# Seven products in place of eight for part of the gate and up projections of a decoder block

## The chip, the cores and the metric

The kernel runs as one launch on one core of a Trainium2 chip. The metric is the device time of one execution in microseconds (us), the median over several runs. The hardware profiler records one execution; its "span" runs from the first instruction to the last. Engines are named as the profile names them: PE is TensorE (matmul), PEld its weight loads, DVE is VectorE, ACT is ScalarE, POOL is GpSimd, SP is SyncE, whose queue issues most DMA transfers.

## The reference

One decoder layer over 256 tokens with 2048 features in float32: a mixer (state space heads and short convolutions), a cross-attention to 256 memory tokens, and a SwiGLU feed-forward network with 5632 hidden features, each with a norm ahead and a residual addition behind, and a final norm. The change is in the feed-forward network:

```
def swiglu(h, w_gate, w_up, w_down):
    return (jax.nn.silu(h @ w_gate) * (h @ w_up)) @ w_down
...
    h = h + swiglu(rmsnorm(h, norm_ffn[i]), w_gate[i], w_up[i], w_down[i])
return rmsnorm(h, norm_final)
```

## The kernel before

*Numbers.* Every float32 operand of a large product is split into a high part (rounded to fp32r) and a low part (what is left). A product is three matmuls: high by high, low by high, high by low. The weights are the moving operand (128 rows by 512 columns), 128x128 blocks of activations the stationary one, so every matmul is preceded by a weight load of an activation block.

*The stream of weights.* `stream_plan` lists all weight tiles in the order of use. A tile, called a chunk here, holds two blocks of 128 input features by 512 output features: 128x1024, 512 KB. Three steps move along that list: `load_to` issues the DMA into a ring of six raw tiles (line 151), `split_to` makes the high part on ScalarE (line 165) and the low part on VectorE (line 166) in rings of four tiles each, and `unit` writes out the matmuls of one or two chunks. `unit` loads up to six chunks ahead and splits up to two chunks past its own; after its first part it advances once each of the processes that are waiting (`step`).

*The order on the engines.* TensorE and SyncE execute in the order written. On ScalarE and VectorE a planner orders the instructions when the program is built; each engine then goes through its list in order.

*Feed-forward network.* The hidden features are in eleven blocks of 512 (`FN`), n = 0 to 10. A block needs eight chunks of the gate weights, `("g", n, c)`, and eight of the up weights, `("u", n, c)`, c = 0 to 7 being pairs of 128 input features. `tok_mm` writes twelve matmuls for a chunk: two feature blocks by two token halves (`tb`) by three, eight with the high weights (lines 238 and 239), then four with the low ones (line 242). They accumulate in PSUM in one bank of 128 tokens by 512 features for each token half; the pool `acc` has four banks, the pool `msc` four more. In blocks 1 to 10 the eight g chunks come first, then the eight u chunks. Two processes follow: `g_post` applies SiLU and the norm's scale on ScalarE, reading the banks (line 1035); `u_post` multiplies by the banks of u on VectorE (line 1043), transposes (line 257), writes the tile to memory (`put`, line 270), reads it back turned (`get`, line 277) and splits it into high and low parts for the down projection (lines 1053 and 1054). `put` and `get` stand in SyncE's queue between the weight loads.

The activations `h2g` are sixteen tiles of 128 features, 256 tokens high part and 256 low part. Those tiles, the finished gate tiles `gs`, the residual `res` and much else are of one size, 128x512 float32, in a pool of 63 called slots.

The down projection runs after block 10 through `d_mm`, also on `tok_mm`.

Of the kernel before, what the change touches and what calls it, by code (L numbers as in the profile page):

```python
# [10 lines left out]
F32 = mybir.dt.float32  # L14
F32R = mybir.dt.float32r
AF = mybir.ActivationFunctionType
ALU = mybir.AluOpType
# [3 lines left out]
T = 256  # L21
D = 2048
KT = D // 128
FF = 5632
FT = FF // 128
FN = FF // 512
H = 32
EPS = 1e-5
NEG = -3.0e38
# [34 lines left out]
            + [(n, c) for n in (2, 3) for c in range(KT)])  # L64


def ffn_order():

    return ([(m, 0, c) for h in range(2) for m in "gu" for c in range(4 * h, 4 * h + 4)]
            + [(m, n, c) for n in range(1, FN) for m in "gu" for c in range(KT // 2)])  # L70


def stream_plan():
# [14 lines left out]
def trunk(tc, wst, vecs, xp, xtp, mp, mtp, wdt_in, nfin, outp):  # L88
    nc = tc.nc
    plan = stream_plan()  # L90
    index = {k: i for i, (k, _) in enumerate(plan)}
    offs, o = [], 0
# [5 lines left out]
    with ExitStack() as ctx:  # L98
# [8 lines left out]
        bp = E(tc.tile_pool(name="blocks", bufs=2))  # L107
        fp = E(tc.tile_pool(name="feat", bufs=3))
# [8 lines left out]
        def nm(s):  # L117
            cnt[0] += 1
            return f"{s}{cnt[0]}"

        def slot(shape=(128, 512), dt=F32):
            return sp.tile(list(shape), dt, tag="s", name=nm("s"))
# [4 lines left out]
        def acc():  # L127
            return accp.tile([128, 512], F32, tag="a", name=nm("a"))

        def msc():  # L130
            return mscp.tile([128, 512], F32, tag="m", name=nm("m"))

        mm = nc.tensor.matmul
        act = nc.scalar.activation
        tt = nc.vector.tensor_tensor
        ts = nc.vector.tensor_scalar
        stt = nc.vector.scalar_tensor_tensor
# [6 lines left out]
        def load_to(n):  # L144
            while nload[0] < min(n, len(plan)):
                i = nload[0]
                w = plan[i][1]
                for f in before.pop(i, ()):
                    f()
                r = rawp.tile([128, 1024], F32, tag="r", name=nm("r"))  # L150
                nc.sync.dma_start(r[:, :w], wst[offs[i]:offs[i] + 128 * w].rearrange("(p n) -> p n", p=128))
                raws[i] = r
                nload[0] += 1

        def split_to(n):
            while nsplit[0] < min(n, len(plan)):
                i = nsplit[0]
                key, w = plan[i]
                r = raws.pop(i)
                h = hip.tile([128, 1024], F32R, tag="h", name=nm("h"))  # L160
                l = lop.tile([128, 1024], F32R, tag="l", name=nm("l"))
                m = 2 if i in (0, 2) else 1
                for j in range(m):
                    c = slice(j * w // m, (j + 1) * w // m)
                    nc.scalar.copy(h[:, c], r[:, c])  # L165
                    tt(l[:, c], r[:, c], h[:, c].bitcast(F32), ALU.subtract)  # L166
                los[i] = l
                his[i] = h
                nsplit[0] += 1
# [60 lines left out]
        def tok_mm(ps, key, blocks, tbs, start, stop, ks=(0, 1)):  # L230


            h, l = fin(key)
            for i in ks:
                w = slice(i * 512, i * 512 + 512)
                for tb in tbs:
                    ah, al = blocks(i, tb)
                    mm(ps[tb], ah, h[:, w], start=start and i == ks[0], stop=False)  # L238
                    mm(ps[tb], al, h[:, w], start=False, stop=False)  # L239
            for i in ks:  # L240
                for tb in tbs:
                    mm(ps[tb], blocks(i, tb)[0], l[:, i * 512:i * 512 + 512], start=False, stop=stop and i == ks[-1])  # L242

        def side_blocks(tiles, k0):

            def blocks(i, tb):
                a = tiles[k0 + i]
                hi, lo = a if isinstance(a, tuple) else (a[:, 0:T], a[:, T:])
                return hi[:, tb * 128:tb * 128 + 128], lo[:, tb * 128:tb * 128 + 128]

            return blocks

        def turn_blocks(src):

            t = bp.tile([128, 1024], F32, tag="b", name=nm("b"))
            for tb in range(2):
                nc.vector.transpose(t[:, tb * 512:tb * 512 + 512], src[tb])  # L257
            return t
# [8 lines left out]
        def put(t):  # L267

            w = drp.tile([2, 128, 512], F32, tag="w", name=nm("w"), bufs=2)
            nc.sync.dma_start(w.rearrange("t p k -> p t k"), t.rearrange("p (t k) -> p t k", t=2))  # L270
            return w
# [14 lines left out]
        def step():  # L286
            alive = []
            cur = list(procs)
            procs.clear()
            for p in cur:  # L290
                try:
                    next(p)
                    alive.append(p)
                except StopIteration:
                    pass
            procs[:0] = alive
# [9 lines left out]
        def unit(parts, post=None):  # L306

            first = [index[k] for k in parts[0][0]]
            last = max([index[k] for ks, _ in parts for k in ks])
            load_to(last + AHEAD - 1)  # L310
            split_to(last + 1)
            for i, (ks, fn) in enumerate(parts):
                fn()
                if i == 0:
                    step()
                    split_to(last + 3)
            load_to(last + AHEAD)
            if post is not None:
                procs.extend(post if isinstance(post, list) else [post])
            now[0] += 1  # L320

        def fin(key):
            i = index[key]
            return his[i], los.get(i)
# [59 lines left out]
        def until(u):  # L384
            while now[0] < u:
                yield
# [36 lines left out]

        dtn = cp.tile([128, 2, H], F32, name="dtn")
        nacs = cp.tile([128, 2, H], F32, name="nacs")
        scr = drp.tile([H, 384], F32, name="acsT")

        def dt_proc():


            yield from until(13)
            w3 = wdt.rearrange("p (k h) -> p k h", h=H)
            tt(w3, w3, vec[:, VOFF["nmix"]:VOFF["nmix"] + KT].unsqueeze(2).to_broadcast([128, KT, H]), ALU.mult)
            yield from until(15)
            ps = msc()
            for kt in range(KT):
                c = kt % 4
                mm(ps[32 * c:32 * c + 32, 0:T], wdt[:, kt * H:kt * H + H],  # L438
                   xraw[kt // 2][:, (kt % 2) * T:(kt % 2) * T + T], start=kt < 4, stop=kt >= 12)
# [98 lines left out]
        first = [[f(), f()] for f in (acc, msc)]  # L538
# [372 lines left out]
        for m, tiles in (("k", mh), ("q", h1g)):  # L911
            accs = [acc(), acc()]
# [57 lines left out]
        h2g = {}  # L970
        h2s = cp.tile([128, 2, 4], F32, name="h2s")
        ff = {}
# [31 lines left out]
        with tc.high_priority():  # L1004
            for mb in range(2):
                Vs.append(slot())
                c = scales["mem"][:, mb:mb + 1]
# [10 lines left out]
        for n in range(4):  # L1018
            accs = [acc(), acc()]
# [6 lines left out]
        gate = {}  # L1026
        gs = {}

        def g_post(n, accs):
            while "r" not in ff:  # L1030
                yield
            gate[n] = []
            for tb in range(2):
                s = gtp.tile([128, 512], F32, tag="g", name=nm("g"))
                act(s, accs[tb], AF.Silu, scale=ff["r"][:, tb:tb + 1])
                gate[n].append(s)

        def u_post(n, accs):
            while n not in gate:
                yield  # L1040
            for tb in range(2):
                s = gate[n][tb]
                stt(s, accs[tb], ff["r"][:, tb:tb + 1], s, ALU.mult, ALU.mult)  # L1043
            t = turn_blocks(gate[n])
            yield
            w = put(t)
            yield
            d = get(w)
            yield
            for i in range(2):  # L1050
                hi, lo = slot(dt=F32R), slot(dt=F32R)
                hv, lv = [a.rearrange("p (f x j) -> p f x j", f=2, x=8) for a in (hi, lo)]
                nc.scalar.copy(hv, d[:, 2 * i:2 * i + 2])  # L1053
                tt(lv, d[:, 2 * i:2 * i + 2], hv.bitcast(F32), ALU.subtract)  # L1054
                gs[2 * n + i] = hi, lo

        def f_mm(accs, m, n, c):
            tok_mm(accs, (m, n, c), side_blocks(h2g, 2 * c), (0, 1), c == 0, c == KT // 2 - 1)

        faccs = {}  # L1060
        order = ffn_order()
        for i in range(0, len(order), 2):
            m, n, c = order[i]
            if c == 0:
                faccs[m, n] = [acc(), acc()]
            parts = [([(m, n, k)], lambda k=k: f_mm(faccs[m, n], m, n, k)) for k in (c, c + 1)]
            p = (g_post if m == "g" else u_post)(n, faccs[m, n]) if c == KT // 2 - 2 else None
            if n == 0:
                unit(parts[:1])
                unit(parts[1:], p)  # L1070
            else:
                unit(parts, p)


        ss = cp.tile([128, 2, 5], F32, name="ss")
# [90 lines left out]
        for n in range(4):  # L1166
            accs = [acc(), acc()]
# [148 lines left out]
```

## Time and profile before

| | |
|---|---|
| median of 3 runs | 1510.32 us (1509.64 to 1510.48) |
| profiled execution, its own time | 1509.91 us |
| its span | 1508.2 us |
| TensorE, busy in the span | 99%, 6733 matmuls |
| VectorE, ScalarE, GpSimd | 61%, 51%, 2% |
| mean granted TensorE clock | 0.999 |
| DMA | 346.68 MB, mean 230 GB/s |

The share of busy time is an average over stages. In a line of a group, the source line, the engine and the operation come first, then the tile written and the tiles read with their shapes, the count, the busy time, the mean of one in ns, and behind the last bar the time in which the engine stood idle just before such an instruction, with what ended most of it. A TensorE matmul's busy time overlaps with that of its neighbours, so its cost is the distance from one start to the next and not the mean duration. In views in order of time a row has its start and its duration in us; several equal instructions in a row are drawn together (x2).

### The profile page before, as it was taken

The numbers are of one execution on the slowest core, as the hardware profiler recorded it, in microseconds if no ns is written. First come the engines' busy times: TensorE is split into PE (matmuls) and PEld (weight loads), VectorE is DVE, ScalarE is ACT, GpSimd is POOL, SyncE is SP. The second block draws the span as 40 slices with busy tenths as digits, with TensorE's granted clock in tenths as the row PEclk, the third lists the DMA queues.
The fourth block names the chain that finished last, engine by engine and source line by source line (L and its number), as shares of the span: only waits on it lengthen the run. The fifth ranks groups of instructions, "written<-read, shape, count | busy, mean of one in ns | idle before, by whom it ended". The sixth has DMA issues, their size and how long they took to land.

```text
span 1508.2 us, 18230 instructions
## 1 busy us (share of the span) xinstructions
PE 1497.8 (99%) x6733; PEld 1234.6 (82%) x6733; DVE 920.9 (61%) x1152; ACT 768.5 (51%) x1033; POOL 34.5 (2%) x46
## 2 busy tenths in 40 slices
PE   9999999999999999999999999999999999999997
PEld 7788888888888888888888888888888888888886
DVE  6677776777785765566675455555545555455453
ACT  7477554757654444454565444444444444344343
POOL 0011000101000000000000000000000000000000
PEclk9999999999999999999999999999999999999999
DMA  9786766868766766776557666666566667666662
GB/s 365 262 290 212 279 243 208 294 226 280 263 220 223 265 212 209 273 265 228 218 189 240 240 218 220 221 221 217 191 218 234 219 220 243 199 195 195 192 191 93
DMA packets 149210, 346.68 MB, mean 230 GB/s; under 512 B 11360, under 2 KB 62976, under 8 KB 149120
## 3 DMA queue, kind: packets, MB, share of 16 engines
q1 hardware_dynamic: 140064, 338.64, 65.7%
q10 hardware_dynamic: 9056, 6.87, 1.6%
q8 instruction: 52, 0.85, 0.2%
q14 instruction: 38, 0.31, 0.1%
HBM read 321.30 MB, written 24.17 MB: 229 GB/s over the span
## 4 chain that ended last, share of the span: by engine, by line
PE 98%; DMA 0%; issue 0%; DVE 0%; SPq 0%; ACT 0%; DVEq 0%; POOLq 0%; POOL 0%
PE a L238 32%; PE a L242 32%; PE a L239 32%; PE m L659 1%; PE m L238 0%; PE m L239 0%; PE m L242 0%; DMA r<-in_w_dram 0%; PE m L966 0%; PE m L661 0%; PE m L643 0%; PE m L935 0%; PE m L438 0%; PE m L954 0%; PE m L617 0%
## 5 line engine op out<-in xcount | busy, mean ns | idle before, releaser
L166 DVE TENSOR_TENSOR l<-r,h 128x1024 fp32r<-128x1024 f32 (+1 forms) x539 | 653.0, 1217 | 481.5 <-ACT h L165 471.4
L165 ACT CAST h<-r 128x1024 fp32r<-128x1024 f32 (+1 forms) x539 | 562.6, 1047 | 595.2 <-PE a L239 554.5
L238 PE MATMUL a<-h,s 128*128 128x512 f32 x2111 | 825.6, 391 | 0.0
L239 PE MATMUL a<-h,s 128*128 128x512 f32 x2111 | 821.8, 389 | 0.0
L242 PE MATMUL a<-l,s 128*128 128x512 f32 x2111 | 568.1, 389 | 0.1
L238 PEld LDWEIGHTS a<-h,s 128*128 128x128 f32 x2111 | 396.6, 188 | 84.3 <-issue 2.0
L242 PEld LDWEIGHTS a<-l,s 128*128 128x128 f32 x2111 | 396.2, 188 | 82.9 <-DVE l L166 0.5
L239 PEld LDWEIGHTS a<-h,s 128*128 128x128 f32 x2111 | 396.6, 188 | 81.3
L257 DVE STREAM_TRANSPOSE b<-s 128x512 f32<-128x512 f32 x62 | 40.6, 688 | 6.8 <-ACT s L264 6.8
L600 DVE SCALAR_TENSOR_TENSOR t<-t,vec,t 128x255 f32<-128x255 f32 (+2 forms) x72 | 32.9, 488 | 5.3 <-ACT t L597 4.6
L264 ACT ACTIVATE s<-a,xr 128x512 f32<-128x512 f32 x42 | 26.4, 680 | 4.0 <-DMA s<-acsT 3.5
L1043 DVE SCALAR_TENSOR_TENSOR g<-a,fscale,g 128x512 f32<-128x512 f32 x22 | 15.5, 746 | 12.0 <-PE a L242 12.0
L180 DVE SCALAR_TENSOR_TENSOR s<-s,vec,s 128x256 fp32r<-128x256 f32 x32 | 14.5, 479 | 5.9 <-ACT s L179 5.9
L815 ACT ACTIVATE s<-f,vec 128x256 fp32r<-128x256 f32 x28 | 12.2, 498 | 11.3 <-DMA f<-w 11.3
L1116 POOL TENSOR_TENSOR fr<-fr,half 128x1 f32<-128x1 f32 x2 | 1.1, 550 | 714.2 <-DVE fr L1115 714.2
L1054 DVE TENSOR_TENSOR s<-f,s 128x512 fp32r<-128x512 f32 x22 | 14.3, 687 | 3.7 <-ACT s L1053 2.5
L816 DVE SCALAR_TENSOR_TENSOR s<-f,vec,s 128x256 fp32r<-128x256 f32 x28 | 12.0, 480 | 7.1 <-ACT s L815 7.1
L582 ACT ACTIVATE s<-s,nacs 128x256 f32<-128x256 f32 x32 | 16.0, 500 | 0.0
L1053 ACT CAST s<-f 128x512 fp32r<-128x512 f32 x22 | 12.5, 618 | 6.5 <-DMA f<-w 6.5
L219 POOL TENSOR_TENSOR rr<-rv,half 128x2 f32<-128x2 f32 x8 | 6.5, 811 | 408.5 <-DVE rv L218 408.5
L179 ACT ACTIVATE s<-s,vec 128x256 fp32r<-128x256 f32 x32 | 15.2, 501 | 1.0 <-DMA s<-in_x_dram 0.4
L399 ACT ACTIVATE s<-s 128x512 f32<-128x512 f32 x16 | 10.1, 631 | 10.8 <-DMA s<-in_mt_dram 5.8
(171 smaller groups left out, 476.7 us busy)
## 6 DMA issues: line engine op xcount, KB each, us to landing
r<-in_w_dram SPq DMA_DIRECT2D x535, 512.0 KB, 4.3
w<-b SPq DMA_DIRECT2D x42, 512.0 KB, 3.3
f<-w SPq DMA_DIRECT2D x42, 512.0 KB, 5.1
s<-acsT ACTq DMA_DIRECT2D x24, 256.0 KB, 5.3
s<-in_xt_dram SPq DMA_DIRECT2D x16, 256.0 KB, 7.4
s<-in_mt_dram SPq DMA_DIRECT2D x8, 256.0 KB, 6.3
s<-in_m_dram SPq DMA_DIRECT2D x8, 256.0 KB, 3.9
s<-in_x_dram SPq DMA_DIRECT2D x7, 256.0 KB, 7.2
```

The source lines that it names most:

```text
L165: nc.scalar.copy(h[:, c], r[:, c])
L166: tt(l[:, c], r[:, c], h[:, c].bitcast(F32), ALU.subtract)
L179: act(a[:, 0:T], src, AF.Identity, scale=gain)
L238: mm(ps[tb], ah, h[:, w], start=start and i == ks[0], stop=False)
L239: mm(ps[tb], al, h[:, w], start=False, stop=False)
L242: mm(ps[tb], blocks(i, tb)[0], l[:, i * 512:i * 512 + 512], start=False, stop=stop and i == ks[-1])
L257: nc.vector.transpose(t[:, tb * 512:tb * 512 + 512], src[tb])
L264: act(o[tb], accs[tb], AF.Identity, scale=r[:, tb:tb + 1])
L582: act(t, t, AF.Exp, bias=b[:, 0:1])
L600: stt(a[:, d:], u[:, 0:T - d], v("cw", 4 * ct + k), a[:, d:], ALU.mult, ALU.add)
L659: mm(yp[64 * i:64 * i + 64, 0:T], xd[:, 0, i, :], f[:, i * T:i * T + T], start=True, stop=False)
L1043: stt(s, accs[tb], ff["r"][:, tb:tb + 1], s, ALU.mult, ALU.mult)
```

## The change

In blocks 1 to 7 (`SEVEN`), two of the eight feature pairs, c = 0 and c = 1, are treated otherwise. For one such pair, the activations are a two by two array of blocks (two feature blocks, two token halves) and the weights another (two feature blocks; g and u). Eight block products made up the result; now there are seven, of sums and differences of blocks, after Strassen's scheme (in Winograd's form), and the results are put together afterwards.

- `ffn_units` gives the new order. A block is: the pair c = 0 of g and u in one part; g2 g3 g4 u2 u3 u4 in three units of two chunks; the pair c = 1; g5 g6 g7 u5 u6 u7. The banks of g and u of a block are now both taken at its start.
- `token_sums` makes, once for each pair, the four sums of activation blocks and splits them into high and low parts (`seven_a`). It is written ahead of the ninth unit of block 0.
- `pair_sums`, called by `split_to` at the u chunk of a pair, makes four sums of weight halves on VectorE, in the raw tiles and one tile more, and splits three of them (128x512) into high and low parts on ScalarE and VectorE. One half of the u raw tile holds a sum when it is split as usual. The raw tile of g is held until then.
- `seven_mm` writes the 21 matmuls in three groups. Four of the products go to four banks of `msc` shared by both pairs, three directly to banks of g and u.
- `p_post` reads the four shared banks after the second pair: one copy on ScalarE, four additions or subtractions on VectorE, into two tiles of the pool `feat`. `whole` adds the result to a bank of g or u (one operation on VectorE for each of the four banks) before SiLU and before the product.

```
+SEVEN = range(1, 8)
...
+def ffn_units():
+    o = [[((m, 0, c),)] for h in range(2) for m in "gu" for c in range(4 * h, 4 * h + 4)]
+    for n in range(1, FN):
+        if n in SEVEN:
+            for q, rest in ((0, "g2 g3 g4 u2 u3 u4"), (1, "g5 g6 g7 u5 u6 u7")):
+                o.append([(("g", n, q), ("u", n, q))])
+                k = [(a[0], n, int(a[1])) for a in rest.split()]
+                o += [[(a,), (b,)] for a, b in zip(k[0::2], k[1::2])]
+        else:
+            o += [[((m, n, c),), ((m, n, c + 1),)] for m in "gu" for c in range(0, KT // 2, 2)]
+    return o
...
+        def pair_sums(nc_, u):
+            g = held.pop(nc_)
+            a, b = slice(0, 512), slice(512, 1024)
+            f = bp.tile([128, 1024], F32, tag="b", name=nm("b"))
+            tt(f[:, a], g[:, a], u[:, a], ALU.add)
+            tt(u[:, a], u[:, a], u[:, b], ALU.add)
+            tt(f[:, b], f[:, a], u[:, b], ALU.add)
+            tt(g[:, a], f[:, b], g[:, b], ALU.add)
+            pair_parts[nc_] = []
+            for x in (f[:, a], f[:, b], g[:, a]):
+                h, l = slot(dt=F32R), slot(dt=F32R)
+                nc.scalar.copy(h, x)
+                tt(l, x, h.bitcast(F32), ALU.subtract)
+                pair_parts[nc_].append((h, l))
...
+                if key in pairs:
+                    if key[0] == "g":
+                        held[key[1:]] = r
+                    else:
+                        pair_sums(key[1:], r)
                 h = hip.tile([128, 1024], F32R, tag="h", name=nm("h"))
...
+        def p_post(n, p):
+            x, y = [fp.tile([128, 1024], F32, tag="f", name=nm("f")) for _ in range(2)]
+            c11, c21, c12, c22 = x[:, 0:512], x[:, 512:], y[:, 0:512], y[:, 512:]
+            nc.scalar.copy(c11, p[0])
+            tt(c22, p[2], c11, ALU.subtract)
+            tt(c12, p[1], c22, ALU.add)
+            tt(c21, p[3], c22, ALU.add)
+            tt(c22, p[1], c21, ALU.add)
+            corr[n] = {("g", 0): (c11, ALU.add), ("g", 1): (c21, ALU.subtract),
+                       ("u", 0): (c12, ALU.add), ("u", 1): (c22, ALU.add)}
...
+        def whole(m, n, tb, ps):
+            if n not in SEVEN:
+                return ps
+            c, op = corr[n][m, tb]
+            tt(c, ps, c, op)
+            return c
...
-                act(s, accs[tb], AF.Silu, scale=ff["r"][:, tb:tb + 1])
+                act(s, whole("g", n, tb, accs[tb]), AF.Silu, scale=ff["r"][:, tb:tb + 1])
...
-                stt(s, accs[tb], ff["r"][:, tb:tb + 1], s, ALU.mult, ALU.mult)
+                stt(s, whole("u", n, tb, accs[tb]), ff["r"][:, tb:tb + 1], s, ALU.mult, ALU.mult)
...
+        def token_sums(c):
+            s0, s1 = h2g[2 * c], h2g[2 * c + 1]
+            x, y = slot(), slot()
+            for i, a in enumerate((s0, s1)):
+                tt(x[:, i * T:i * T + T], a[:, 0:T].bitcast(F32), a[:, T:].bitcast(F32), ALU.add)
+            a11, a21, a12, a22 = [x[:, i * 128:i * 128 + 128] for i in range(4)]
+            o = [y[:, i * 128:i * 128 + 128] for i in range(4)]
+            tt(o[0], a21, a22, ALU.subtract)
+            tt(o[1], a11, o[0], ALU.subtract)
+            tt(o[2], a21, a11, ALU.subtract)
+            tt(o[3], a12, o[1], ALU.subtract)
+            h, l = slot(dt=F32R), slot(dt=F32R)
+            nc.scalar.copy(h, y)
+            tt(l, y, h.bitcast(F32), ALU.subtract)
+            seven_a[c] = [(h[:, i * 128:i * 128 + 128], l[:, i * 128:i * 128 + 128]) for i in range(4)]
...
+        def seven_mm(n, c):
+            g, u, p = faccs["g", n], faccs["u", n], shared[n]
+            gh, gl = fin(("g", n, c))
+            uh, ul = fin(("u", n, c))
+            t1, t2, t4 = pair_parts.pop((n, c))
+            a, b = slice(0, 512), slice(512, 1024)
+            raw = side_blocks(h2g, 2 * c)
+            sa = seven_a[c]
+            for group in (((p[0], raw(0, 0), (gh[:, a], gl[:, a])), (g[0], raw(1, 0), (gh[:, b], gl[:, b]))),
+                          ((p[3], sa[2], (uh[:, a], ul[:, a])), (p[1], sa[0], t1)),
+                          ((p[2], sa[1], t2), (g[1], raw(1, 1), t4), (u[0], sa[3], (uh[:, b], ul[:, b])))):
+                for ps, (ah, al), (bh, bl) in group:
+                    mm(ps, ah, bh, start=c == 0, stop=False)
+                    mm(ps, al, bh, start=False, stop=False)
+                for ps, (ah, al), (bh, bl) in group:
+                    mm(ps, ah, bl, start=False, stop=c == 1 and any(ps is q for q in p))
...
+        for i, parts in enumerate(ffn_units()):
+            if i == 8:
+                for c in range(2):
+                    token_sums(c)
+            post = []
+            for part in parts:
+                m, n, c = part[0]
+                for k in part:
+                    if k[2] == 0:
+                        faccs[k[:2]] = [acc(), acc()]
+                if len(part) == 2:
+                    if c == 0:
+                        shared[n] = [msc() for _ in range(4)]
+                    else:
+                        post.append(p_post(n, shared[n]))
+                elif c == KT // 2 - 1:
+                    post.append((g_post if m == "g" else u_post)(n, faccs[m, n]))
+            unit([(list(part), lambda part=part: part_mm(part)) for part in parts], post or None)
```

More of the change, by code (lines that the diff above doesn't have):

```diff
@@ L64, in out_order @@
             + [(n, c) for n in (2, 3) for c in range(KT)])
+def ffn_units():
[9 more added lines that the diff above has]
+    return o
 def ffn_order():
-    return ([(m, 0, c) for h in range(2) for m in "gu" for c in range(4 * h, 4 * h + 4)]
-            + [(m, n, c) for n in range(1, FN) for m in "gu" for c in range(KT // 2)])
+    return [k for u in ffn_units() for part in u for k in part]
 def stream_plan():
@@ L153, in load_to @@
                 nload[0] += 1
+        held, pair_parts = {}, {}
+        pairs = {k for u in ffn_units() for part in u if len(part) == 2 for k in part}
+        def pair_sums(nc_, u):
[12 more added lines that the diff above has]
+                pair_parts[nc_].append((h, l))
         def split_to(n):
@@ L237, in tok_mm @@
                     ah, al = blocks(i, tb)
-                    mm(ps[tb], ah, h[:, w], start=start and i == ks[0], stop=False)
+                    first = start if isinstance(start, bool) else tb in start
+                    mm(ps[tb], ah, h[:, w], start=first and i == ks[0], stop=False)
                     mm(ps[tb], al, h[:, w], start=False, stop=False)
@@ L1027, in trunk @@
         gs = {}
+        corr = {}
+        def p_post(n, p):
[8 more added lines that the diff above has]
+                       ("u", 0): (c12, ALU.add), ("u", 1): (c22, ALU.add)}
+            return
+            yield
+        def whole(m, n, tb, ps):
[4 more added lines that the diff above has]
+            return c
         def g_post(n, accs):
@@ L1055, in u_post @@
                 gs[2 * n + i] = hi, lo
[L1057 to L1072, printed above, removed]
+        faccs, shared, seven_a = {}, {}, {}
@@ new lines, in part_mm @@
+        def part_mm(part):
+            m, n, c = part[0]
+            if len(part) == 2:
+                seven_mm(n, c)
+                return
+            start = c == 0
+            if n in SEVEN:
+                start = (1,) if (m, c) == ("u", 2) else False
+            tok_mm(faccs[m, n], part[0], side_blocks(h2g, 2 * c), (0, 1), start, c == KT // 2 - 1)
+        for i, parts in enumerate(ffn_units()):
[4 more added lines that the diff above has]
+            for part in parts:
+                m, n, c = part[0]
+                for k in part:
+                    if k[2] == 0:
+                        faccs[k[:2]] = [acc(), acc()]
+                if len(part) == 2:
+                    if c == 0:
[5 more added lines that the diff above has]
+            unit([(list(part), lambda part=part: part_mm(part)) for part in parts], post or None)
```

## The prediction

> **What bounds the kernel now.** I read the page's busy line, slices and chain first, then the stretch of the seven blocks that change, by windows, and last the order in time inside it.
>
> ```profile
> span 1508.2 us, 18230 instructions
> PE 1497.8 (99%) x6733; PEld 1234.6 (82%) x6733; DVE 920.9 (61%) x1152; ACT 768.5 (51%) x1033; POOL 34.5 (2%) x46
> PEclk9999999999999999999999999999999999999999
> PE 98%; DMA 0%; issue 0%; DVE 0%; SPq 0%; ACT 0%; DVEq 0%; POOLq 0%; POOL 0%
> PE a L238 32%; PE a L242 32%; PE a L239 32%; PE m L659 1%; PE m L238 0%; PE m L239 0%; PE m L242 0%; DMA r<-in_w_dram 0%; PE m L966 0%; PE m L661 0%; PE m L643 0%; PE m L935 0%; PE m L438 0%; PE m L954 0%; PE m L617 0%
> L166 DVE TENSOR_TENSOR l<-r,h 128x1024 fp32r<-128x1024 f32 (+1 forms) x539 | 653.0, 1217 | 481.5 <-ACT h L165 471.4
> L165 ACT CAST h<-r 128x1024 fp32r<-128x1024 f32 (+1 forms) x539 | 562.6, 1047 | 595.2 <-PE a L239 554.5
> L242 PE MATMUL a<-l,s 128*128 128x512 f32 x2111 | 568.1, 389 | 0.1
> ```
>
> The chain is TensorE for 98% at full clock, in lines 238, 239 and 242, with no idle time. VectorE waits for ScalarE's cast, and the cast for TensorE to give a buffer back: both run ahead as far as four buffers allow. So a matmul taken out is worth its spacing, unless its operands come late. The seven blocks:
>
> ```profile
> core 0: us, PE busy (x) PEld busy (x) DVE busy (x) ACT busy (x) POOL busy (x), PEclk, DMA share, GB/s
> 830.00:1134.00 304.00, 304.00 (x1343) 251.81 (x1342) 162.41 (x154) 133.24 (x140) 0.00 (x0) 1.00 0.64 217
> L1043 DVE SCALAR_TENSOR_TENSOR g<-a,fscale,g x22: 740/746/751, 824.9 to 1260.8; 128x512 f32<-128x512 f32 x22
> 1101.49 1.07 PE L242 MATMUL a<-l,s 128*128 128x512 f32 x4
> 1101.68 1.05 ACT L165 CAST h<-r 128x1024 fp32r<-128x1024 f32 x1 [1.67 <-PE a L239]
> 1102.39 0.39 PE L238 MATMUL a<-h,s 128*128 128x512 f32 x1
> 1102.77 1.22 DVE L166 TENSOR_TENSOR l<-r,h 128x1024 fp32r<-128x1024 f32 x1 [1.50 <-ACT h L165]
> 1104.21 1.07 PE L242 MATMUL a<-l,s 128*128 128x512 f32 x4
> ```
>
> *Spacing.* From one L242 to the next is 2.72 us for the 12 matmuls of a chunk (one weight tile): 226.7 ns each. A block (16 chunks, 192 matmuls) lasts 43.52 us.
>
> *Slack.* The cast at 1101.68 waited for the last h matmul of the chunk that ended at 1102.39, so it fills the buffer of the fourth chunk after, which starts at 1102.39 + 3 x 2.72 = 1110.55. It ends at 1102.73: 7.8 us early. The low part ends at 1103.99 and is first read eight matmuls in, at 1112.36: 8.4 us early. This slack pays for bursts on VectorE.
>
> *VectorE and ScalarE.* 162.41 of 304 us and 133.24 of 304 us: 23.25 and 19.07 us a block.
>
> **The change part by part.**
>
> *Removed: matmuls.* For two of a block's eight feature pairs, g and u chunks cost 2 x 12 matmuls; the seven products cost 7 x 3 = 21. That is 3 x 2 x 7 = 42 fewer, each still with its own weight load: 42 x 0.2267 = 9.52 us. A block lasts 186 x 0.2267 = 42.17 us.
>
> *Added: vector and scalar work in a block.* Two times seven 128x512 operations (four sums, three low parts), four in p_post, four corrections: 22 on VectorE. ScalarE gets seven 128x512 copies.
>
> ```profile
> L1054 DVE TENSOR_TENSOR s<-f,s 128x512 fp32r<-128x512 f32 x12 | 7.8, 687 | 1.2 <-PE a L242 0.9 <-ACT s L1053 0.2
> L1053 ACT CAST s<-f 128x512 fp32r<-128x512 f32 x12 | 6.8, 618 | 2.2 <-DMA f<-w 2.2
> L1091 DVE TENSOR_TENSOR s<-a,s x6: 683/688/692, 1317.5 to 1440.7; 128x512 f32<-128x512 f32 x6
> 1127.25 1.22 DVE L166 TENSOR_TENSOR l<-r,h 128x1024 fp32r<-128x1024 f32 x1 [1.50 <-ACT h L165]
> 1129.57 1.41 DVE L1043 SCALAR_TENSOR_TENSOR g<-a,fscale,g 128x512 f32<-128x512 f32 x2 [1.09 <-PE a L242]
> 1130.89 1.29 DVE L257 STREAM_TRANSPOSE b<-g 128x512 f32<-128x512 f32 x2
> 1132.11 2.31 DVE L166 TENSOR_TENSOR l<-r,h 128x1024 fp32r<-128x1024 f32 x2
> L257 DVE STREAM_TRANSPOSE b<-g 128x512 f32<-128x512 f32 x12 | 7.8, 685 | 0.0
> ```
>
> The same operation takes 0.687 us from SBUF (L1054) and 0.688 from PSUM (L1091). Back to back its price is lower: two transposes of 0.685 end after 1.29, so the second starts 0.605 after the first. Above, the sums depend on each other; I allow the 0.04 us by which a low part follows its cast (1102.73 to 1102.77): 0.727. So VectorE gets 13.3 to 16.0 us more, 36.6 to 39.3 of 42.17: 87% to 93%. ScalarE gets 7 x 0.618 = 4.3, 23.4 in all. I take 0.66, 37.8 us: still short of the bound, so on average the work is hidden beside TensorE.
>
> The Trainium skill, "VectorE: DVE Perf Modes", section "The DRAIN you can't avoid", has it that the next operation does not start until the pipe is empty, with or without a semaphore: by that rule the spacing is the whole 0.687, and a block has 38.4 us of VectorE work; the transposes, 80 ns closer than that, do not bear it out. Either way the sum stays.
>
> *Inside the block.* Take the end of chunk u7 as 0 and let VectorE and ScalarE go in the order written, which is unfavourable. Chunk g7 ended at -8.16; its two corrections end at -6.8, the SiLUs at -6.1, the cast of the next g0 at -5.1, its low part at -3.9; seven sums and low parts (7 x 0.66) at 0.7; the low part of u0 at 1.9, needed after ten matmuls, at 2.3. The first correction, which gives the bank of u back, ends at 2.5; the seven-product unit wants that bank at its 17th matmul, 3.6. The rest of u_post (0.687 + 2 x 0.746 + 2 x 0.685) ends near 6.0, the low part of g2 at 7.1; it is needed at 29 x 0.2267 = 6.6. So this order loses about 0.55 us a block; in the second half p_post falls into 16 us of ordinary chunks and loses nothing. But the trace does not follow the order written: the low part at 1127.25 comes ahead of the SiLU product at 1129.57, which stands before it in the text. Work goes when ready. The sums need only raw tiles, which land well ahead, so I take 0, and keep 7 x 0.55 = 3.9 us for the range.
>
> *Waits on SyncE.* The transposes start 1.4 us later for the two new corrections, more with a backlog; put waits for them, and weight loads queue behind it.
>
> ```profile
> SPq L270 <- DVE b L257: 48.7, 8, 6.1
> 1125.78 0.33 SPq L151 DMA_DIRECT2D r<-in_w_dram  x1
> 1132.21 0.38 SPq L270 DMA_DIRECT2D w<-b  x1
> 1132.68 1.29 SPq L151 DMA_DIRECT2D r<-in_w_dram  x2
> DMA to landing us min/median/max: 3.1/3.3/7.5
> 1142.48 1.06 ACT L165 CAST h<-r 128x1024 fp32r<-128x1024 f32 x1 [0.63 <-PE a L239]
> ```
>
> The load at 1132.68 takes the buffer of the tile split at 1127.25 and is itself the sixth after it, cast at 1142.48; it lands near 1136.0, 6.5 us ahead of a cast that is 7.8 us ahead: 14 us cover some 6 us of later put. The held gate tile (freed after the sums instead of after its low part, about 5 us) has the same cover. Cost 0.
>
> *Buffers.* No DMA is added or taken away, and GpSimd's queue is not touched. The four shared banks are read by p_post right after the second seven-product unit (one cast, four sums: 3.4 us) and wanted again 16.3 us after that unit's end, six ordinary chunks later; the banks of g are free at -6.8. Of the 63 slots, block 7 takes the most: 16 features, 8 residuals, 28 finished gate tiles, 4 token sums and 6 weight sums, 62. One set of weight sums fits, a second one ahead of it would wait for the first; sets are 21 us apart, so cost 0.
>
> *token_sums, once, halfway through block 0.* Twice: two 128x256 sums, four 128x128, one low part of 128x512. With 0.42 for 256 columns, 0.15 (two columns) to 0.42 for 128, and 0.687: 4.3 to 6.4 us of VectorE.
>
> ```profile
> L1109 DVE TENSOR_TENSOR s<-a,s 128x256 f32<-128x256 f32 x3 | 1.2, 420 | 5.9 <-PE a L242 4.0 <-PE a L1163 1.8
> L1100 DVE TENSOR_REDUCE pre<-ss 128x2 f32<-128x6 f32 x1 | 0.2, 153 | 0.0
> 797.37 1.68 DVE L816 SCALAR_TENSOR_TENSOR s<-f,vec,s 128x256 fp32r<-128x256 f32 x4 [3.41 <-ACT s L815]
> 804.40 0.89 DVE L816 SCALAR_TENSOR_TENSOR s<-f,vec,s 128x256 fp32r<-128x256 f32 x2 [2.54 <-ACT s L815]
> 805.74 1.23 DVE L166 TENSOR_TENSOR l<-r,h 128x1024 fp32r<-128x1024 f32 x1 [0.45 <-ACT h L165]
> ```
>
> Here the splits already run late: the low part at 805.74 belongs to a chunk whose buffer came back at 800.3 (block 0 starts 16 x 2.72 before 824.9, at 781.3; its seventh chunk ends 7 x 2.72 later), 5.4 of its slack gone. With 6.4 more it would be 3.3 us too late; in the idle 3.41 and 2.54 us it costs nothing. It needs no transfer of that moment, so I take 0.5 with all small stalls.
>
> *Sum.* 1509.91 (span 1508.2 and 1.7 around it) - 9.52 + 0.5 = 1500.9. The median of the runs is 0.4 above the profiled run: 1501.3.
>
> **The rivals.**
>
> *Program order wins, or token_sums stalls.* 3.9 us, and up to 3.3 once: 1504.7 to 1508, near 1506. For it: the 93% end; against: the order at 1127.25.
>
> *VectorE becomes the bound.* From (42.17 - 23.25) / 22 = 0.86 us an operation. At 0.90 a block lasts 43.05: the gain is 7 x 0.47 = 3.3, 1507; at 0.92 nothing is left. Against: no row of such an operation passes 0.75.
>
> *A bank of PSUM, not faster but slower.* Before, g and u of the next block open their banks 21.8 us apart; now g and u are opened in one unit, and u waits 3.6 us after u7 for u_post's first read. If that read stands behind all seven sums (4.8), the low part of u0 (1.22) and itself (0.69), it ends at 6.7: 3.1 late, 7 x 3.1 = 21.7, giving 1522. It decides from 9.5 / 7 = 1.36 us, a read that ends 5.0 us after u7. For it: 87% of VectorE is taken; against: the sums are ready before u7 ends.
>
> *The change frees less than the spacing.* If the weight load, 188 ns, were the true price, 42 x 0.188 = 7.9, and 1502.9.
>
> ```profile
> L242 PEld LDWEIGHTS a<-l,s 128*128 128x128 f32 x2111 | 396.2, 188 | 82.9 <-DVE l L166 0.5
> ```
>
> The Trainium skill, "TensorE: Matmul & The Clock Gate", "Back-to-back issue gap", gives about 131 ns for such a stream at 512 columns: 5.5 us, 1505.3 as an estimate of that page. The measured 226.7 ns speaks against it; its chance is part of this rival's.
>
> **How the numbers follow.** About 0.2% (3 us) is what can be told from no change. Forecast 0.60; program order or token_sums 0.24; freed less 0.03; VectorE the bound, with a result within 3 us, 0.06; the bank 0.07. The first three are faster: 0.87; same 0.06; slower 0.07. The range takes them in: 1500.0 (0.5 of stalls gone, and the scatter of the runs, 0.8) to 1507.5.
>
> **What would show it.** Matmuls down by 42, the spacing 226.7 ns; VectorE in the seven blocks at 87% to 93%; TensorE idle under 1 us before the seven-product units and before the low part of g2. Wrong if these show idle of 0.5 us or more in each block, if u's opening matmul waits for a correction, or if the new operations exceed 0.75 us.

## The result and the profile after

The changed kernel takes 1500.63 us (median of 4, 1500.12 to 1500.95) against 1510.3 us beside it: a ratio of 0.9936, 95% interval 0.9919 to 0.9954. Forecast: 1501.3, range 1500.0 to 1507.5. The profiled execution took 1500.12 us, 9.8 less than the one before.

The page after, the parts that answer to those shown of before:

```profile
span 1498.4 us, 18385 instructions
PE 1488.0 (99%) x6691; PEld 1226.5 (82%) x6691; DVE 1016.0 (68%) x1320; ACT 796.3 (53%) x1084; POOL 35.3 (2%) x46
PE 99%; issue 0%; DMA 0%; SPq 0%; ACT 0%; DVE 0%; DVEq 0%; POOLq 0%; POOL 0%
```

6733 matmuls have become 6691, 42 fewer. The chain is still TensorE, 99%, and VectorE is busy for 68% of the span in place of 61%. The next views are the stretch of the seven blocks, one block of it, and VectorE in order of time where that block begins. A row of a stretch gives its length, the busy time and the count of PE, PEld, DVE, ACT and POOL, the granted clock, the DMA share and GB/s:

```profile
830.00:1120.00 290.00, 290.00 (x1281) 240.15 (x1280) 242.13 (x294) 155.69 (x185) 0.00 (x0) 1.00 0.66 227
909.00:951.16 42.16, 42.16 (x187) 34.91 (x186) 35.91 (x45) 22.58 (x28) 0.00 (x0) 1.00 0.64 225
905.66 0.68 DVE L190 TENSOR_TENSOR s<-r,s 128x512 fp32r<-128x512 f32 x1
906.73 1.23 DVE L209 TENSOR_TENSOR l<-r,h 128x1024 fp32r<-128x1024 f32 x1 [0.39 <-ACT h L208]
909.00 1.29 DVE L1094 TENSOR_TENSOR f<-a,f 128x512 f32<-128x512 f32 x2 [1.04 <-PE a L286]
910.21 1.41 DVE L1111 SCALAR_TENSOR_TENSOR g<-f,fscale,g 128x512 f32<-128x512 f32 x2
912.75 3.45 DVE L209 TENSOR_TENSOR l<-r,h 128x1024 fp32r<-128x1024 f32 x3
951.16 1.29 DVE L1094 TENSOR_TENSOR f<-a,f 128x512 f32<-128x512 f32 x2 [1.05 <-PE a L286]
```

The corrections that read the banks of u (L1094) start at 909.00 and again at 951.16: a block lasts 42.16 us, the 186 matmuls at 226.7 ns of the prediction to 0.01. VectorE even waits there, 1.04 us, for the last matmul of u7: its sums and their low parts are done by then, the last (L190) at 906.34. The product u0 of the new block may write its bank 3.6 us after that matmul; both corrections have ended after 1.3. The low part at 906.73, of g2, stands ahead of u_post.

### The profile page after: what moved, and what is told of

Same layout as the page of the kernel before. It is cut to its first block, busy times and chain, and to the rows that moved or that the text cites. A ratio compares the mean times of both kernels' runs of the same rounds, so it can differ in the third digit from the quotient of the medians.

```text
span 1498.4 us, 18385 instructions
## 1 busy us (share of the span) xinstructions
PE 1488.0 (99%) x6691; PEld 1226.5 (82%) x6691; DVE 1016.0 (68%) x1320; ACT 796.3 (53%) x1084; POOL 35.3 (2%) x46
## 4 chain that ended last, share of the span: by engine, by line
PE 99%; issue 0%; DMA 0%; SPq 0%; ACT 0%; DVE 0%; DVEq 0%; POOLq 0%; POOL 0%
PE a L282 30%; PE a L283 30%; PE a L286 30%; PE m L1157 1%; PE m L1160 1%; PE m L1158 1%; PE a L1158 1%; PE a L1160 1%; PE a L1157 1%; PE m L703 1%; PE m L283 0%; PE m L286 0%; PE m L282 0%; DMA r<-in_w_dram 0%; PE m L1010 0%
## 5 line engine op out<-in xcount | busy, mean ns | idle before, releaser
L282 PE MATMUL a<-h,s 128*128 128x512 f32 x1999 | 781.9, 391 | 0.2 <-ACT h L208 0.2
L283 PE MATMUL a<-h,s 128*128 128x512 f32 x1999 | 778.1, 389 | 0.0
L286 PE MATMUL a<-l,s 128*128 128x512 f32 x1999 | 538.0, 389 | 0.0
L282 PEld LDWEIGHTS a<-h,s 128*128 128x128 f32 x1999 | 375.4, 188 | 80.2 <-issue 2.0
L286 PEld LDWEIGHTS a<-l,s 128*128 128x128 f32 x1999 | 375.2, 188 | 78.2
L283 PEld LDWEIGHTS a<-h,s 128*128 128x128 f32 x1999 | 375.4, 188 | 77.0
L1094 DVE TENSOR_TENSOR f<-a,f 128x512 f32<-128x512 f32 x28 | 18.0, 684 | 7.8 <-PE a L286 7.8
L189 ACT CAST s<-b 128x512 fp32r<-128x512 f32 x28 | 16.7, 617 | 4.5 <-DVE b L182 3.6
L190 DVE TENSOR_TENSOR s<-b,s 128x512 fp32r<-128x512 f32 x28 | 18.7, 684 | 0.0
L182 DVE TENSOR_TENSOR b<-r,r 128x512 f32<-128x512 f32 x14 | 9.7, 690 | 11.0 <-DMA r<-in_w_dram 11.0
```

Of the source, the lines that this page charges most:

```text
L190: tt(l, x, h.bitcast(F32), ALU.subtract)
L282: mm(ps[tb], ah, h[:, w], start=first and i == ks[0], stop=False)
```

## The experiments

Each is an edit of the changed kernel. Their times stand beside the 1500.63 us of the changed kernel and the kernel before, 1510.15 to 1510.35 in the runs beside them.

**e1: the matmuls put back, the vector work kept.**

```
...
             sa = seven_a[c]
+            for _ in range(6 if c == 0 else 0):
+                mm(p[0], raw(0, 0)[0], gh[:, a], start=True, stop=True)
...
```

> All vector work of the change is kept, and each of the seven blocks gets six more 128x512 matmuls at its start, into a shared bank that the next product overwrites: the count is that of the kernel before. Theory (a matmul is worth its spacing, the vector work is hidden): 42 x 0.2267 = 9.5 us more than the changed kernel, 1510.1, the time of the kernel before. Rival (the gain has another source, the order of the chunks or the banks taken at the start): well under 1510, near 1500.6 if the count has no part in it. Rival (the vector work costs something beside TensorE): over 1510.5.

Measured: 1509.93 us, 1.000 of the kernel before (0.999 to 1.001). Six matmuls a block bring back 9.3 us, 0.22 us each. The count is the whole gain; the order of the chunks, the banks and 12 us a block of vector work cost nothing that can be seen.

**e2: the vector work left out, the matmuls kept.**

```
-                        pair_sums(key[1:], r)
+                        held.pop(key[1:])
...
-            t1, t2, t4 = pair_parts.pop((n, c))
+            t1, t2, t4 = (gh[:, a], gl[:, a]), (gh[:, b], gl[:, b]), (uh[:, a], ul[:, a])
```

with p_post and the corrections empty; token_sums stays.

> The 21 matmuls of each pair stay, but the weight sums, p_post and the corrections are left out (the products run on unsummed halves, and the shared banks are read by nobody). VectorE falls from 35.9 to about 23.3 us a block. Theory: the 12.6 us a block were wholly hidden, so the time stays at 1500.6, within 0.5. Rival (small waits in each block, program order in part): 1 to 4 us less.

Measured: 1500.86 us (1500.58 to 1501.22). VectorE fell from 242.13 to 158.31 us in the same 290, and the time did not. So it was hidden, all of it:

```profile
830.00:1120.00 290.00, 290.00 (x1282) 240.19 (x1280) 158.31 (x149) 130.79 (x139) 0.00 (x0) 1.00 0.68 227
```

**e3: the order written, in place of the planner's.**

```
...
+            if parts[0][0][1] in SEVEN:
+                written.enter_context(tc.manual_schedule(engines={mybir.EngineType.Activation, mybir.EngineType.DVE}))
...
```

> In the seven blocks VectorE and ScalarE execute in the order in which the kernel is written, in place of the planner's; nothing else differs. The prediction's rival: the low part of g2 then ends 0.55 us late in each block, behind the seven sums and the whole of u_post: 7 x 0.55 = 3.9 us more, near 1504.5, with the idle time of TensorE ahead of the matmul that reads g2's low part. Rival (the slack absorbs it in any order): 1500.6.

Measured: 1503.49 us (1502.79 to 1505.02), 2.9 us more. In the profiled executions (1502.79 and 1500.12) 0.7 us of the difference lies ahead of the changed blocks: the first SiLU product of u_post, in block 0, starts at 825.4 in place of 824.7. From there to the last one, in block 10, 428.3 us pass in place of 426.3: 2.0 us, 0.3 a block. VectorE, and the two groups of matmuls of a block that read late parts, in order of time:

```profile
910.44 0.68 DVE L1094 TENSOR_TENSOR f<-a,f 128x512 f32<-128x512 f32 x1
911.04 1.22 DVE L209 TENSOR_TENSOR l<-r,h 128x1024 fp32r<-128x1024 f32 x1
912.31 0.50 PE L1160 MATMUL m<-l,s 128*128 128x512 f32 x1
912.65 0.39 PE L1160 MATMUL m<-s,s 128*128 128x512 f32 x1
915.45 3.45 DVE L209 TENSOR_TENSOR l<-r,h 128x1024 fp32r<-128x1024 f32 x3
916.75 1.13 PE L286 MATMUL a<-l,s 128*128 128x512 f32 x4
```

The low part of u0, behind the first correction (L1094), ends at 912.26; its matmul starts at 912.31, and the next one 0.34 later in place of 0.227. That of g2, behind the whole of u_post, ends near 916.67 and its matmuls start at 916.75, 1.13 for four in place of 1.07. These are the two places that the prediction named as the tightest, but not with the weight that it gave them: from start to start of the matmuls, 1.3 of the 2.0 us are lost at the low parts of the seven-product units' u chunks (L1160) and 0.2 at those of g2 (L286); the rest is spread over the matmuls behind them. The rival was real; the planner's order is what kept it away.

**e4 and e5: more work for VectorE**, four or eight operations behind each set of sums:

```
...
+            for _ in range(4):
+                tt(f[:, a], f[:, b], f[:, b], ALU.add)
...
```

e5 has `range(8)`.

> Four more 128x512 additions on VectorE behind each set of weight sums, on a tile that nobody reads after: eight a block. VectorE goes from 35.9 us a block to 35.9 + 8 x 0.6 = 40.7 of 42.17. Theory (average load below the block's time is hidden, whatever the bursts): 1500.6 to 1502. Rival (bursts matter before the average does): waits in each block, 1503 to 1510.

> Eight more 128x512 additions on VectorE behind each set of weight sums, sixteen a block: 35.9 + 16 x 0.6 = 45.5 us of work for 42.17 us of matmuls. Theory (VectorE becomes the bound once a block's work passes the block's matmuls): 7 x 3.3 = 23 us more, near 1524, slower than the kernel before. Rival (the slack of four buffers carries over from block to block): under 1515.

Measured: 1502.76 us (1500.32 to 1503.58), between the two forecasts, and 1530.06 us (1527.46 to 1531.96). The windows of both, and TensorE's waits, with their sum in us, their count and the longest:

```profile
830.00:1120.00 290.00, 289.23 (x1275) 238.88 (x1274) 271.01 (x348) 154.05 (x184) 0.00 (x0) 1.00 0.67 227
PE a L1159 <- DVE f L1096: 0.8, 1, 0.8
PE a L285 <- DVE s L862: 0.6, 1, 0.6
```

```profile
830.00:1100.00 270.00, 253.97 (x1090) 207.85 (x1089) 259.81 (x345) 132.91 (x158) 0.00 (x0) 0.97 0.60 207
926.65:973.06 46.41, 42.45 (x186) 34.83 (x186) 45.09 (x61) 22.72 (x27) 0.00 (x0) 1.00 0.59 204
PE a L288 <- DVE l L211: 19.5, 6, 4.0
```

At 93% of VectorE the view lists two single waits. One is the product u0 waiting for the first correction (L1159 behind L1096), the prediction's bank, in one block of seven. The other (L285) lies in block 0, ahead of the stretch: the last low parts of the activations (L862), which stand behind token_sums, came late. This is the execution of 1503.51 us; matmul by matmul it loses 1.3 us in the changed blocks against the changed kernel's, 1.2 in block 0, and 0.9 ahead of block 0, where nothing differs. The fastest of the four, 1500.32, can have lost next to nothing, so how much of the 2.1 us between the medians is the load's stays open.

In e5 VectorE is the bound: from one of its waits to the next (926.65 to 973.06) it is busy for 45.09 us, more than the 42.17 that a block's matmuls take. The kernel is 1.3% slower than before the change. The expected 1524 was too low: 19.5 us are waits, and 0.97 in the clock column tells of the rest (see the last section).

**e6: three pairs** of eight in blocks 1 to 6, two in block 7.

```
-SEVEN = range(1, 8)
+PAIRS = {1: 3, 2: 3, 3: 3, 4: 3, 5: 3, 6: 3, 7: 2}
...
+          2: "0 g2g3 g4u2 u3u4 1 g5g6 g7u5 u6u7",
+          3: "0 g3g4 u3u4 1 g5u5 2 g6g7 u6u7",
...
```

The second table gives the order of a block's chunks by its number of pairs, and token_sums is made for the third pair too. e7 to e10 use the same tables.

> Three feature pairs of eight by seven products in blocks 1 to 6, two in block 7: 20 in place of 14, 18 matmuls fewer, 4.1 us. VectorE has 7 x 0.6 more a block, 40.1 us, and the block's matmuls last 41.5: 97%. Theory (hidden as long as the average is below): 1496.5, with the small waits that 93% showed (2 us), 1498.5. Rival (bursts decide at 97%): 1500 or more, no gain over two pairs.

Measured: 1497.21 us (1496.96 to 1497.48), 0.9914 of the kernel before (0.9899 to 0.9929), 3.4 us better than two pairs. The forecast had 4.1; the profiled execution is 0.8 us late ahead of the changed blocks (the first SiLU product at 825.5 in place of 824.7). TensorE has no idle time with VectorE at 94%:

```profile
830.00:1100.00 270.00, 270.00 (x1193) 223.65 (x1192) 254.04 (x324) 158.96 (x195) 0.00 (x0) 1.00 0.66 233
```

**e7 and e8: the weight sums on GpSimd**, with two pairs, and with four in blocks 1 to 6, two in block 7, one in block 8.

```
...
-            tt(f[:, a], g[:, a], u[:, a], ALU.add)
+            gtt(f[:, a], g[:, a], u[:, a], op=ALU.add)
...
```

and so for the other three sums.

> The changed kernel with the four weight sums of each pair on GpSimd in place of VectorE. VectorE falls by 8 x 0.6 to 31.1 us a block. No row shows such a sum on GpSimd; the nearest, 128x2, takes 0.8 us. If one takes up to 2.5 us, a chain of four is done within the 21 us between pairs, and the time stays at 1500.6. Rival (GpSimd and VectorE slow each other down, or the chain of four comes late): 1502 to 1515, with longer VectorE operations or TensorE idle ahead of the products of t1, t2 and t4.

> Weight sums on GpSimd, and four pairs in blocks 1 to 6, two in block 7, one in block 8: 27 pairs in place of 14, 39 matmuls fewer, 8.8 us. VectorE has 23.3 + (12 + 8) x 0.6 = 35.3 of 40.8 us a block. Theory: 1491.8, faster than both kernels. Rival (as for the two pairs on GpSimd, with four chains of four sums in 40.8 us): 1495 and more.

Measured: 1504.66 and 1572.75 us: the theory fell, twice. The groups of e7 in the stretch 830 to 1100, and its matmuls' waits:

```profile
L215 DVE TENSOR_TENSOR l<-r,h 128x1024 fp32r<-128x1024 f32 x102 | 134.0, 1343 | 29.5 <-ACT h L214 29.3
L196 DVE TENSOR_TENSOR s<-b,s 128x512 fp32r<-128x512 f32 x24 | 22.8, 953 | 0.0
L190 POOL TENSOR_TENSOR b<-b,r 128x512 f32<-128x512 f32 x13 | 19.1, 1469 | 0.0
L1100 DVE TENSOR_TENSOR f<-a,f 128x512 f32<-128x512 f32 x24 | 15.3, 680 | 0.0
PE a L1163 <- DVE f L1100: 0.8, 2, 0.6
PE a L1163 <- DVE g L1117: 0.8, 1, 0.8
```

A sum on GpSimd takes 1.3 to 1.5 us on average, and VectorE's operations on two SBUF tiles become longer where they run beside one: the low parts of the sums in tile b take 953 ns in place of 687 on average, the splits 1343 in place of 1217. The corrections, which read one operand from PSUM, take 680, but in e7 none of them runs beside a sum. In e8 some do:

```profile
931.03 1.28 DVE L1100 TENSOR_TENSOR f<-a,f 128x512 f32<-128x512 f32 x2
931.26 1.28 POOL L191 TENSOR_TENSOR r<-b,r 128x512 f32<-128x512 f32 x1 [6.62 <-DVE l L215]
934.25 1.59 POOL L189 TENSOR_TENSOR r<-r 128x512 f32<-128x512 f32 x1
934.64 4.51 DVE L215 TENSOR_TENSOR l<-r,h 128x1024 fp32r<-128x1024 f32 x2
935.80 2.26 POOL L190 TENSOR_TENSOR b<-b,r 128x512 f32<-128x512 f32 x1
```

Two corrections beside a sum take 1.28 us, alone 1.29 (909.00 in the changed kernel), and the sum 1.28; two splits take 4.51 in place of 2.31, and the sums beside them up to 2.26. The Trainium skill has this rule ("SBUF — State Buffer", section "Who interferes with whom"): a VectorE instruction with two SBUF inputs contends with a GpSimd instruction that reads SBUF, one with at most one SBUF input does not. The rows of e8 agree on both sides. Part of the work moved to GpSimd is paid on VectorE: in the stretch 830 to 1100 its busy time falls from 229.36 us in the changed kernel to 217.23 in e7, 1.9 us a block in place of the 4.8 expected.

Nearly all that TensorE loses in the changed blocks of e7 is lost at the opening of u0's product (L1163), the bank of the prediction's rival. It waits for block 0's SiLU product once (L1117) and for the first correction else (L1100). In the longest of these, at 1042.79, that correction stands behind the last low part of the sums, which follows GpSimd's fourth sum, and behind the split of u0. Whether the late sum or the longer operations weigh more was not separated. With four pairs, sums of 1.5 to 1.9 us came late in every block, and with them the low parts on VectorE:

```profile
L190 POOL TENSOR_TENSOR b<-b,r 128x512 f32<-128x512 f32 x27 | 51.2, 1897 | 0.0
L191 POOL TENSOR_TENSOR r<-b,r 128x512 f32<-128x512 f32 x27 | 41.2, 1526 | 116.4 <-DVE l L215 64.1 <-issue 51.9
PE m L1166 <- DVE l L215: 18.4, 8, 3.2
PE a L1166 <- DVE s L196: 14.9, 10, 2.6
```

**e9 and e10: the three pairs again**, with one pair more in block 8, and with the order written as in e3.

> The version with three pairs in blocks 1 to 6 and two in block 7, and one pair more in block 8: 21 pairs, 63 matmuls fewer than in the kernel before. Theory: 63 x 0.2267 = 14.3 us under the kernel before, 1495.9 to 1496.5 with what three pairs showed. Rival (block 8 waits for slots held by block 7): 1497.2 or more.

> Three pairs, with VectorE and ScalarE in the order written in blocks 1 to 7, as was tried with two pairs (2.8 us more there). Theory (it is the planner's order that keeps late operands away, and it counts for more the fuller VectorE is): over 1497.2 + 2.8, 1501 to 1510, with TensorE late at low parts behind the sums. Rival (at 94% any order does): 1497 to 1500.

Measured: 1495.91 us (1495.57 to 1496.07), 0.9906 of the kernel before (0.9889 to 0.9922), as expected from the count and the fastest version here; and 1532.95 us (1529.68 to 1535.14), 35.7 us more than the same work in the planner's order. e10's windows of 5 us where a block begins, ScalarE in order of time there, and TensorE's waits in the changed blocks:

```profile
915.00:920.00 5.00, 2.21 (x6) 1.19 (x6) 5.00 (x8) 4.41 (x5) 0.00 (x0) 0.74 0.07 25
920.00:925.00 5.00, 5.00 (x14) 3.94 (x15) 5.00 (x7) 1.05 (x1) 0.00 (x0) 0.57 0.95 329
915.55 0.62 ACT L195 CAST s<-r 128x512 fp32r<-128x512 f32 x1 [0.58 <-DVE r L191]
916.07 3.88 ACT L214 CAST h<-r 128x1024 fp32r<-128x1024 f32 x4
PE m L1163 <- ACT h L214: 12.3, 6, 2.1
PE m L1166 <- DVE l L215: 6.0, 6, 1.4
```

In each of six blocks the high part of a seven-product unit's u chunk is 2.1 us late: its cast (916.07) stands behind the copy of the last sum (915.55), which waited for that sum (L191). The low part is up to 1.4 later still; while TensorE waits, VectorE is full (5.00 of 5.00). My expectation had the sign and not the size, and it looked for the wait at the low parts alone: 12.3 of the 18.3 us lie ahead of the high ones.

## Why the prediction was right

*The matmuls.* 42 fewer at 226.7 ns each, 9.52 us. The first SiLU product of u_post, in block 0, starts at 824.9 before and 824.7 after, the last, in block 10, at 1260.8 and 1251.0: 435.9 us become 426.3, 9.6 less, and 0.2 of the 9.8 lies ahead of the changed blocks. e1 shows that nothing else contributes. That a matmul frees less than its spacing (the 188 ns of its weight load) is excluded: block time and count give 226.7 on both sides. The 131 ns that the Trainium skill gives ("TensorE: Matmul & The Clock Gate", section "Back-to-back issue gap") appear in no run here.

*The cover.* Forecast 0.5 us of stalls, measured none (e2). The half microsecond, and the 0.2 ahead of the changed blocks, make up the 0.7 between 1501.3 and 1500.63. The 0.2 is chance: it was in no term, and e2, e3 and e4, the same kernel up to block 0, lie 0.7 to 1.1 us behind the changed kernel there.

*VectorE's load was over-sized.* I took 0.66 us an operation, 37.8 us a block, with 36.6 (87%) as the lower end; a block shows 35.91 (85%), (35.91 - 23.25) / 22 = 0.575 an operation. About half of the difference to 37.8 lies in the 22 new operations, 0.62 each on average, counted from the end of the one before. The other half, a term left out, is in the work that was there already: three splits behind one another end after 3.45 us, 1.115 from one to the next, where alone they take 1.22. A fuller VectorE is cheaper by the operation, and the room was larger than the prediction had it: e6 used it. The section of the Trainium skill that the prediction sets against such distances ("VectorE: DVE Perf Modes", "The DRAIN you can't avoid") also says that a next operation which is not held starts earlier, so it does not rule them out.

*The order.* The planner's order, not the text, sets it, as the prediction took from one pair of rows of before; that was thin evidence for seven blocks. e3 and e10 show what the other order costs. The walk in the order written gave 0.55 us a block at g2's low part and a margin of 0.4 at u0's; measured 0.3 a block, most of it at u0's. The walk had the first correction behind u0's low part; in e3 it stands ahead of it (910.44) and takes the margin.

*token_sums.* 4.3 to 6.4 us of VectorE were to go into idle time in block 0. The changed kernel's trace has a 128x128 sum at 0.29 us and no idle TensorE there:

```profile
L1136 DVE TENSOR_TENSOR s<-s,s 128x128 f32<-128x128 f32 x2 | 0.6, 288 | 0.0
```

The prediction looked at the splits alone; e4 shows a tighter edge, the activations' own low parts behind token_sums.

*The bank.* The wait did not occur in the changed kernel (1.3 against 3.6 us). It is a true edge: the view lists it once in e4 and three times in e7.

## What to carry to other kernels

Where one engine is the whole chain and never idle, price a removed instruction at its start-to-start distance, and judge added work on another engine by two things: its share of the new block time, and the latest moment at which each result may come. The share alone misleads: the same work that cost nothing in the planner's order, with VectorE at 94%, cost 35.7 us in the order written. Before moving work to an idle engine, look whether the two engines' operations become longer beside each other.

## What the hardware showed that I had not expected

A wait can cost more than its length. TensorE in e10 where a block begins:

```profile
914.73 0.39 PE L1166 MATMUL a<-l,s 128*128 128x512 f32 x1
917.16 0.59 PE L1163 MATMUL m<-h,s 128*128 128x512 f32 x1 [2.05 <-ACT h L214]
917.55 0.63 PE L1164 MATMUL m<-h,s 128*128 128x512 f32 x1
...
919.77 0.80 PE L1166 MATMUL m<-l,s 128*128 128x512 f32 x1 [0.73 <-DVE l L215]
...
924.47 0.39 PE L288 MATMUL a<-h,s 128*128 128x512 f32 x1
```

After 2.05 us of idle time a matmul takes 0.63 us and the next one starts 0.43 later, in place of 0.227; this holds for about 7 us, some 15 matmuls, and the granted clock of those windows is 0.74 and 0.57. So a block pays its wait, 18.3 / 6 = 3.05 us, and 15 x 0.2 = 3 us more; six blocks about 36, near the 35.7 measured. In the same way the 19.5 us of e5's waits became 29.4, while e4's waits of 0.8 and 0.6 us left the clock at 1.00. The Trainium skill ("TensorE: Matmul & The Clock Gate", section "Why this matters for your kernels") asks for no idle gap over about 3 us between bursts of matmuls; here gaps of 2.05 us lowered the clock in five of e10's six blocks, and two gaps of 2.74 us in e5 did not. So the length of a gap does not decide it alone. In the traces of e5, e8 and e10 every change of the granted clock lies on a grid of 3.41 us. Three steps of that grid in e10 and three in e5 (around the wait that ends at 926.65):

```profile
866.23:869.64 3.41, 1.76 (x8) 1.13 (x6) 3.41 (x7) 2.12 (x4) 0.00 (x0) 1.00 0.00 0
869.64:873.06 3.42, 1.63 (x6) 1.05 (x7) 3.42 (x6) 3.19 (x4) 0.00 (x0) 1.00 0.16 40
873.06:876.47 3.41, 3.41 (x10) 2.64 (x9) 3.41 (x5) 0.34 (x1) 0.00 (x0) 0.50 0.88 308
921.83:925.24 3.41, 2.08 (x10) 1.39 (x8) 3.41 (x6) 0.72 (x1) 0.00 (x0) 1.00 0.01 2
925.24:928.66 3.42, 2.01 (x9) 1.67 (x10) 3.42 (x4) 1.05 (x1) 0.00 (x0) 1.00 0.66 216
928.66:932.07 3.41, 3.41 (x17) 2.83 (x16) 3.41 (x4) 1.05 (x1) 0.00 (x0) 1.00 0.89 292
```

With TensorE idle for 1.79 of 3.42 us (869.64) the next step runs at half the clock; with 1.65 (866.23) it does not, and e5's wait, split into 1.33 and 1.41, leaves the clock at 1.00. Between 820 and 1300 us of the three traces all 18 steps at full clock with 1.79 us or more of idle time were followed by half clock, and no step with 1.75 or less was. What decides is thus the idle share of a step, about half, as far as these traces go; ends of matmuls are modelled, and no run moved a wait against the grid.

The price of a sum on GpSimd, 1.3 to 1.9 us on average for 128x512 against 0.69 on VectorE, was in no row of before either.
